# A hybrid decoder step in fp32-grade products: w_o split beside the last S products, transpositions in the rounded 32-bit type, smaller DMA scratch

## The chip, the cores and the metric

One Trainium2 chip; the kernel runs on one of its cores. The metric is device time in microseconds (us), the median of several runs. Engines are called as in the profile: PE is TensorE, PEld its weight loads, DVE VectorE, ACT ScalarE, POOL GpSimd, SP SyncE. L12 is line 12 of the kernel before, unless the change is spoken of.

## The reference, cut to what matters

1024 prompt tokens and 64 sample tokens (8 x 8), model width 1024, inner width 2048, 32 heads in 4 groups, state 128, chunks of 128 tokens. All values are 32-bit floats.

```python
proj = h @ w_in                       # h: normed, conditioned x
u_pool, z_pool, z_ssm, xbc, dt_raw, g_raw = split(proj)
p = (pool_mix(u_pool) * silu(z_pool)) @ w_pool_out
...                                   # causal conv, then per chunk and group:
cb  = einsum('bign,bjgn->bijg', C, B)
att = cb[..., None] * decay * dt
y   = einsum('bijge,bjgep->bigep', att, x) + C @ (exp(acs) * h)
h   = h * exp(last) + einsum('bjgn,bjge,bjgep->bgepn', B, w_in, x)
...
s = rmsnorm((y + D * x) * silu(z_ssm), ssm_norm_g) @ w_ssm_out
m = sigmoid(g_pool) * p + sigmoid(g_ssm) * s
x = x + gate * (m @ w_o)              # then the final rmsnorm
```

## The kernel before, in words

**Split products.** A full-precision product is made of three products in the rounded 32-bit type (F32R, "fp32r" in the profile; TensorE takes it in one pass, while a plain 32-bit product shows as two passes): each operand is split into a high part (its rounded copy, made by ACT) and a low part (the rest, a subtraction on DVE or POOL), and high x high, high x low and low x high are accumulated. `gemm_` (L348 to L356) does this for one 128-row output tile in blocks of 384, 352 and 352 columns (1088 tokens), three matmuls for each 128 of depth; its PSUM tiles `mm` come from a pool of three. A transposition on TensorE is a matmul whose stationary operand is the data and whose streamed operand is an identity matrix.

**Stages.** Up to about 830 us: projections, convolution and the samples' recurrence. From about 832 to 1120 us the chunk stage: 4 groups x 8 chunks of the recurrence (`chunk`), woven with the products that don't need the last group: 8 units of P (`P_unit`, with w_pool_out) and 24 units of S for groups 0 to 2 (`S_unit`, with w_ssm_out). From about 1122 us the tail: 8 units of S for group 3 (`tail_unit`), then the product with w_o (8 row tiles of 48 matmuls and the sample rows), about 1204 to 1291 us, and the final norm.

**A chunk.** SP loads x, B, C (`xb`) and the decays (`dec`); ACT takes exponentials of dec (L1196, L1392, the latter for `cE`), POOL masks it (L1187). TensorE transposes four tiles of x (L1400) and one of B (L1402) and multiplies B by C (L1403, a plain 32-bit product). ACT copies B's high part (`bt`, L1406) and, once DVE has scaled x (L1412, L1413), the high part of x (`xw`, L1415). DVE multiplies dec and cE by the product of B and C (L1416, L1418) and makes the low parts `xwl` (L1419) and `btl` (L1420). Then TensorE makes the outputs of the heads (`inner`, L1208 with dec, L1211 with cE) and the new state (L1429 to L1431), and `finish` gates the output and splits it for the S products (L1362 to L1373).

**Split of w_o, before.** From the 14th chunk on, `wo_splits` runs between the steps of the chunks in 16 halves of 128 x 512: SP loads a half into `pw` (2 buffers), ACT copies its high part into `ph` (1 buffer, L1674) and issues its store to HBM (L1675), POOL subtracts in place (L1676), and SP stores the low part (L1670). In the tail `wo_prep` (L1761, L1762) loads both parts of each of the 8 row blocks again.

**A tail unit.** After the three blocks of unit m, `m_done` (L1783) has DVE add the block to the sums of groups 0 to 2 (L1795), multiply by the gain (sigmoid gate times the row norm, `r`, L1788, then L1800) and POOL add P's part (L1801; DVE does it for m = 7). `m_split` splits the result m for the last product: ACT copies (L1779), DVE subtracts (L1780), and L1768 and L1769 do the same for the 64 sample columns `sh`. `samples[m]` are four matmuls of 512 columns with w_o for the sample rows (L1774).

**Order.** Each engine works in order. A scheduler sets each engine's order from the program by priorities; `in_line` chains the instructions of the named engines in program order instead. In the chunk stage it holds for TensorE; `high_priority(PRIO)` moves work ahead in the scheduler.

Of the kernel before, what the change touches and what calls it, by code (L numbers as in the profile page):

```python
# [8 lines left out]
F32 = mybir.dt.float32  # L9
# [37 lines left out]
def tile_pool_ssd_step(  # L47
# [65 lines left out]
    make_identity(nc, ident)  # L113
    blk = const([NS, NB], "blk")
# [1267 lines left out]
    def chunk(g, c):  # L1382
# [16 lines left out]
        for q in range(4):  # L1399
            nc.tensor.transpose(px[:, q * P:(q + 1) * P], xb[:, q], ident)  # L1400
        pbc = PB()
        nc.tensor.transpose(pbc[:, :P], Bf, ident)  # L1402
# [258 lines left out]
    wo_d = [dram(f"wo{k}", [P, 2, D]) for k in range(8)]  # L1661

    def wo_splits():
        raws = {}
        for n in range(18):
            if n < 16:
                raws[n] = ck.tile([P, 512], F32, tag="pw", name=nm("pw"), bufs=2)
                load(raws[n], w_o[0, n // 2 * P:n // 2 * P + P, n % 2 * 512:n % 2 * 512 + 512])
            if n > 1:
                load(wo_d[(n - 2) // 2][:, 1, n % 2 * 512:n % 2 * 512 + 512], raws.pop(n - 2))  # L1670
            yield
            if n < 16:
                hi = ck.tile([P, 512], F32R, tag="ph", name=nm("ph"), bufs=1)
                act(hi, raws[n], AF.Copy)  # L1674
# [3 lines left out]
    wos = wo_splits()  # L1678
# [16 lines left out]
    for i in range(len(seq)):  # L1695
        if i > 12:
            next(wos, None)
# [6 lines left out]
        if i > 12:  # L1704
            next(wos, None)
# [10 lines left out]
    for it in (pc_, wos):  # L1716
        for _ in it:
            pass
# [8 lines left out]
    mq = open_("mq", 5)  # L1727
# [16 lines left out]
    rstd = [PB() for _ in range(3)]  # L1744
    for c in range(9):
# [3 lines left out]
        mm(rstd[c // 4][:, c % 4 * P:c % 4 * P + n], ones[:n, :], dg, start=True, stop=True)  # L1749
# [6 lines left out]
    def wo_prep(k, mem):  # L1756
# [4 lines left out]
        load(hi.bitcast(F32), wo_d[k][:, 0])  # L1761
        load(lo.bitcast(F32), wo_d[k][:, 1])  # L1762
# [20 lines left out]
    def m_done(m):  # L1783
        r = R()
        load(r, gs_d[m])
        for j, ps in enumerate(rstd):
            s = slice(512 * j, min(512 * j + 512, T))
# [158 lines left out]
```

## Time and profile before

| what | value |
|---|---|
| median of 3 runs | 1298.56 us (1297.77 to 1300.59) |
| profiled execution, span | 1297.1 us |
| PE busy | 1255.9 us (97%) |
| DVE / ACT / POOL busy | 910.5 (70%) / 708.8 (55%) / 677.4 (52%) us |
| DMA traffic | 251.70 MB, mean 194 GB/s |
| HBM read / written | 167.06 MB / 83.01 MB |
| chunk stage, first and last transposition of x | 832.8 and 1102.2 us |

A row of the timeline reads: start in us, length in us, engine, line, operation, output<-inputs by the program's names, shapes, number of like instructions joined in the row, and in brackets the time that the engine stood idle before it and what ended that. Rows of groups give the count, then busy us and mean ns of one, then the idle time before them and its releasers. Matmuls overlap, so their cost is read from start to start. The median lies 1.46 us above the profiled span.

### The profile page before, as it was taken

The numbers are of one execution on the slowest core, as the hardware profiler recorded it, in microseconds if no ns is written. First come the engines' busy times: TensorE is split into PE (matmuls) and PEld (weight loads), VectorE is DVE, ScalarE is ACT, GpSimd is POOL, SyncE is SP. The second block draws the span as 40 slices with busy tenths as digits, with TensorE's granted clock in tenths as the row PEclk, the third lists the DMA queues.
The fourth block names the chain that finished last, engine by engine and source line by source line (L and its number), as shares of the span: only waits on it lengthen the run. The fifth ranks groups of instructions, "written<-read, shape, count | busy, mean of one in ns | idle before, by whom it ended". The sixth has DMA issues, their size and how long they took to land.

```text
span 1297.1 us, 26554 instructions
## 1 busy us (share of the span) xinstructions
PE 1255.9 (97%) x9771; PEld 1173.9 (90%) x9771; DVE 910.5 (70%) x1580; ACT 708.8 (55%) x1684; POOL 677.4 (52%) x563
## 2 busy tenths in 40 slices
PE   7999999999999999999999999999998999999998
PEld 6779999989999999999889999889998999999786
DVE  4685778866979578775777665488676888576433
ACT  4665356375656564545455453687987868201111
POOL 1007668677869776664344444276776747314000
PEclk9999999999999999999999999999999999999999
DMA  9837345465455544444656555999988656575631
GB/s 326 259 107 224 119 150 173 142 202 170 146 180 197 165 155 133 161 135 129 181 158 173 152 178 164 356 355 354 338 270 262 202 168 199 172 266 159 226 106 52
DMA packets 233795, 251.70 MB, mean 194 GB/s; under 512 B 31265, under 2 KB 177905, under 8 KB 233658
## 3 DMA queue, kind: packets, MB, share of 16 engines
q1 hardware_dynamic: 161568, 171.60, 42.1%
q10 hardware_dynamic: 72098, 78.41, 17.5%
q8 instruction: 77, 1.26, 0.4%
q14 instruction: 52, 0.43, 0.1%
HBM read 167.06 MB, written 83.01 MB: 193 GB/s over the span
## 4 chain that ended last, share of the span: by engine, by line
PE 67%; issue 8%; DMA 8%; DVE 6%; POOL 5%; ACT 4%; SPq 0%; ACTq 0%; POOLq 0%; DVEq 0%
PE ps L603 6%; PE ps L604 6%; PE ps L605 6%; PE mm L603 6%; PE mm L605 6%; PE mm L604 6%; PE mm L355 3%; PE mm L356 3%; PE mm L354 3%; PE ps L1208 2%; PE ps L1892 2%; PE ps L1894 2%; PE ps L1893 2%; POOL wlo L163 2%; PE ps L1211 2%
## 5 line engine op out<-in xcount | busy, mean ns | idle before, releaser
L163 POOL TENSOR_TENSOR wlo<-rawA,whi 128x512 fp32r<-128x512 f32 x120 | 184.0, 1538 | 185.6 <-ACT whi L160 101.6
L163 POOL TENSOR_TENSOR wlo<-raw,whi 128x512 fp32r<-128x512 f32 x92 | 150.7, 1646 | 125.3 <-ACT whi L160 91.1
L354 PE MATMUL mm<-Y,whi 128*128 128x352 f32 (+1 forms) x480 | 160.1, 334 | 0.7 <-DVE G L1795 0.5
L355 PE MATMUL mm<-Y,whi 128*128 128x352 f32 (+1 forms) x480 | 157.3, 328 | 1.0 <-DVE Y L1466 1.0
L356 PE MATMUL mm<-Y,wlo 128*128 128x352 f32 (+1 forms) x480 | 156.9, 327 | 0.0
L605 PE MATMUL mm<-Y,wlo 128*128 128x272 f32 x496 | 143.6, 290 | 3.9 <-POOL wlo L163 3.1
L603 PE MATMUL ps<-Y,whi 128*128 128x272 f32 x496 | 144.5, 291 | 2.3 <-ACT o L803 1.7
L603 PE MATMUL mm<-Y,whi 128*128 128x272 f32 x496 | 146.5, 295 | 0.2
L604 PE MATMUL ps<-Y,whi 128*128 128x272 f32 x496 | 143.1, 289 | 0.0
L604 PE MATMUL mm<-Y,whi 128*128 128x272 f32 x496 | 142.9, 288 | 0.0
L605 PE MATMUL ps<-Y,wlo 128*128 128x272 f32 x496 | 142.6, 288 | 0.0
L160 ACT ACTIVATE whi<-rawA 128x512 fp32r<-128x512 f32 x125 | 78.2, 626 | 95.6 <-PE ps L604 44.9
L1051 DVE SCALAR_TENSOR_TENSOR GA<-GA,cvT,GA 128x1112 f32<-128x1112 f32 x72 | 127.1, 1769 | 0.6 <-ACT GA L1048 0.5
L160 ACT ACTIVATE whi<-raw 128x512 fp32r<-128x512 f32 x96 | 58.7, 626 | 91.4 <-DVE raw L549 41.7
L605 PEld LDWEIGHTS mm<-Y,wlo 128*128 128x128 f32 x496 | 93.4, 188 | 5.8 <-POOL wlo L163 4.2
L603 PEld LDWEIGHTS ps<-Y,whi 128*128 128x128 f32 x496 | 93.3, 188 | 4.0 <-ACT o L803 1.9
L603 PEld LDWEIGHTS mm<-Y,whi 128*128 128x128 f32 x496 | 93.3, 188 | 2.5 <-issue 0.8
L604 PEld LDWEIGHTS mm<-Y,whi 128*128 128x128 f32 x496 | 93.4, 188 | 0.7 <-issue 0.6
L604 PEld LDWEIGHTS ps<-Y,whi 128*128 128x128 f32 x496 | 93.3, 188 | 0.3 <-issue 0.2
L605 PEld LDWEIGHTS ps<-Y,wlo 128*128 128x128 f32 x496 | 93.4, 188 | 0.2 <-issue 0.2
L354 PEld LDWEIGHTS mm<-Y,whi 128*128 128x128 f32 x480 | 90.3, 188 | 3.2 <-DVE G L1795 1.4
L355 PEld LDWEIGHTS mm<-Y,whi 128*128 128x128 f32 x480 | 90.3, 188 | 3.2 <-DVE Y L1466 1.6
(452 smaller groups left out, 3851.6 us busy)
## 6 DMA issues: line engine op xcount, KB each, us to landing
rawA<-in_w_in SPq DMA_DIRECT2D x46, 512.0 KB
dec<-acs_d SPq DMA_DIRECT2D x32, 512.0 KB
xbc<-GA ACTq DMA_DIRECT2D x24, 512.0 KB
xb<-xbc SPq DMA_DIRECT2D x32, 384.0 KB
rawA<-in_w_in SPq DMA_DIRECT2D x32, 256.0 KB
pw<-in_w_ssm_out ACTq DMA_DIRECT2D x32, 256.0 KB
ws<-ph ACTq DMA_DIRECT2D x32, 256.0 KB
ws<-pw SPq DMA_DIRECT2D x32, 256.0 KB
```

What stands on the lines that cost most here:

```text
L160: ins = act(hi[:, :, :ncols], raw[:, :, :ncols], AF.Copy)
L163: (eng or nc.gpsimd).tensor_tensor(lo[:, :, :ncols], raw[:, :, :ncols], hi[:, :, :ncols].bitcast(F32), ALU.subtract)
L354: mm(ps[:, :n], a, rh[k][:, o:o + n], start=(k == 0), stop=False)
L355: mm(ps[:, :n], a, rl[k][:, o:o + n], start=False, stop=False)
L356: mm(ps[:, :n], b, rh[k][:, o:o + n], start=False, stop=(k == nk - 1))
L603: mm(p, hi, ah, start=(k == 0), stop=False)
L604: mm(p, hi, al, start=False, stop=False)
L605: mm(p, lo, ah, start=False, stop=(k == 3))
L1051: V.scalar_tensor_tensor(d[:, :n], rp[:, k:k + n], cvT[:, 24 * k + mc:24 * k + mc + 1], d[:, :n], ALU.mult, ALU.add)
L1208: mm(o[hh], xd[:S, 2 * q + hh, :], dec[:S, 2 * q + hh], start=True, stop=state is None)
L1211: mm(o[hh], state[:, h * 64:h * 64 + 64], cE[:, h], start=False, stop=True)
L1892: mm(ps[:, :cw], mhk, wo[k][0][:, s], start=(k == 0), stop=False)
```

## The change

Five things change.

1. `wo_splits` and its 8 MB of HBM buffers go. In the tail, unit m loads the raw 128 x 1024 rows of block m of w_o into an M tile (`wo_load`), and for m < 6 ACT copies the high part and POOL subtracts the low one (`wo_split`); blocks 6 and 7 follow after the units, with block 7's subtraction on DVE.
2. The transpositions of x and B in the chunk stage are declared in the rounded 32-bit type (`turn_r`), data, identity and output alike, with an identity of its own made by POOL at the start. The transpositions of the state (L1239, L1448) stay as they are.
3. The scratch memory for DMA descriptors is 1024 instead of 16384 bytes for each partition, and the pool M of 4352-byte tiles in the tail has 8 buffers instead of 5. The diagonals of the norms lie in one M tile instead of four small ones.
4. The gain (three instructions on DVE) is made when the last block of a unit is there, for m < 7, instead of ahead of the unit's products in the program.
5. In the tail TensorE and DVE are held to program order. The split of m comes one unit later, and the sample products two units later, without their high priority.

```diff
+    identR = const([P, P], "identR", F32R)
+    nc.gpsimd.tensor_copy(identR, ident)
+    def turn_r(out, src):
+        nc.tensor.transpose(out.bitcast(F32R), src.bitcast(F32R), identR)
...
-            nc.tensor.transpose(px[:, q * P:(q + 1) * P], xb[:, q], ident)
+            turn_r(px[:, q * P:(q + 1) * P], xb[:, q])
...
-        nc.tensor.transpose(pbc[:, :P], Bf, ident)
+        turn_r(pbc[:, :P], Bf)
...
-    def wo_splits():
-        raws = {}
-        for n in range(18):
-            if n < 16:
-                raws[n] = ck.tile([P, 512], F32, tag="pw", name=nm("pw"), bufs=2)
-                load(raws[n], w_o[0, n // 2 * P:n // 2 * P + P, n % 2 * 512:n % 2 * 512 + 512])
-            if n > 1:
-                load(wo_d[(n - 2) // 2][:, 1, n % 2 * 512:n % 2 * 512 + 512], raws.pop(n - 2))
-            yield
-            if n < 16:
-                hi = ck.tile([P, 512], F32R, tag="ph", name=nm("ph"), bufs=1)
-                act(hi, raws[n], AF.Copy)
-                store_(wo_d[n // 2][:, 0, n % 2 * 512:n % 2 * 512 + 512], hi.bitcast(F32))
-                nc.gpsimd.tensor_tensor(raws[n].bitcast(F32R), raws[n], hi.bitcast(F32), ALU.subtract)
-            yield
...
-    mq = open_("mq", 5)
+    mq = open_("mq", 8)
...
-        dg = sm.tile([P, P], F32, tag="stc", name=nm("dg"), bufs=4)[:n, :n]
+        dg = dgs[:n, c * P:c * P + n]
...
+    def wo_load(k):
+        raws[k] = M((P, D))
+        load(raws[k], w_o[0, k * P:(k + 1) * P, :])
+
+    def wo_split(k, mem):
         if k < 4:
             hi, lo = w4[0][:, k, :D], w4[1][:, k, :D]
         else:
             hi, lo = mem((P, D), F32R), mem((P, D), F32R)
-        load(hi.bitcast(F32), wo_d[k][:, 0])
-        load(lo.bitcast(F32), wo_d[k][:, 1])
+        raw = raws.pop(k)
+        act(hi, raw, AF.Copy)
+        (V if k == 7 else nc.gpsimd).tensor_tensor(lo, raw, hi.bitcast(F32), ALU.subtract)
...
-            if m < 5:
-                wo_prep(m, M)
-            if m < 7:
-                m_split(m, M8 if m < 4 else G)
-            if m < 5:
-                with tc.high_priority(PRIO):
-                    samples[m]()
+            wo_load(m)
+            if m < 6:
+                wo_split(m, M)
+            if m > 0:
+                m_split(m - 1, M8 if m < 5 else G)
+            if m > 1:
+                samples[m - 2]()
+    in_line((mybir.EngineType.PE, mybir.EngineType.DVE), True)
     run_units([tail_unit(m) for m in range(8)])
...
-    for k in (5, 6):
-        wo_prep(k, late)
-        samples[k]()
-    wo_prep(7, late)
+    for k in (6, 7):
+        wo_split(k, late)
+    samples[6]()
     m_split(7, late)
+    in_line((mybir.EngineType.PE, mybir.EngineType.DVE))
...
-    nc = _bacc.Bacc("TRN2", target_bir_lowering=False, num_devices=1)
+    nc = _bacc.Bacc("TRN2", target_bir_lowering=False, num_devices=1, dynamic_dma_scratch_size=1024)
```

The rows below are the order of one engine, before and after, with the tiles' buffer numbers; "x5" is five like instructions in a row. First ACT in the chunk stage, around the first chunk of group 2, where S products of group 0 are made (G is their sum, L1636 its copy from PSUM; the other names are those of a chunk). Before:

```order
L1674 ACTIVATE ph_14588<-pw_14542 128x512
L1636 ACTIVATE G_13145<-mm_13146 128x384
L1196 ACTIVATE dec_13114<-dec_13114,acT 128x128 x5
L1636 ACTIVATE G_13145<-mm_13190 128x352
L1196 ACTIVATE dec_13114<-dec_13114,acT 128x128 x3
L1675 DMA wo_11233<-ph_14588 128x512
L1406 ACTIVATE bt_13173<-ps_13170 128x128
L1674 ACTIVATE ph_14720<-pw_14674 128x512
L1415 ACTIVATE xw_13179<-ps_13165 128x512
L1423 ACTIVATE xD_13299<-xb_13112,Dv 128x128 x4
L1675 DMA wo_11234<-ph_14720 128x512
```

After (lines six further down in the code):

```order
L1642 ACTIVATE G_13127<-mm_13128 128x384
L1202 ACTIVATE dec_13096<-dec_13096,acT 128x128 x8
L1642 ACTIVATE G_13127<-mm_13169 128x352
L1412 ACTIVATE bt_13152<-ps_13149 128x128
L1421 ACTIVATE xw_13158<-ps_13144 128x512
L1429 ACTIVATE xD_13271<-xb_13094,Dv 128x128 x4
```

The copy of w_o's half that stood between the copies bt and xw, and the two store issues, are gone; the rest keeps its order. Second, POOL in the tail, from the addition of unit 0 on (G is a unit's sum, m P's part). Before:

```order
L1801 TENSOR_TENSOR G_12288<-G_12288,m_15440 128x1088
L1801 TENSOR_TENSOR G_12415<-G_12415,m_15508 128x1088
L1801 TENSOR_TENSOR G_12570<-G_12570,m_15576 128x1088
L1801 TENSOR_TENSOR G_12696<-G_12696,m_15644 128x1088
L1849 TENSOR_TENSOR half_15985<-ident 128x64 x2
L1801 TENSOR_TENSOR G_12883<-G_12883,m_15712 128x1088
L1801 TENSOR_TENSOR G_13015<-G_13015,m_15782 128x1088
```

After (L1753 is the subtraction of w_o, its outputs Y for blocks 0 to 3 and m for 4 and 5; L1796 the addition):

```order
L1753 TENSOR_TENSOR Y_15298<-m_15360,Y_15297 128x1024
L1753 TENSOR_TENSOR Y_15298<-m_15419,Y_15297 128x1024
L1796 TENSOR_TENSOR G_12282<-G_12282,m_15311 128x1088
L1753 TENSOR_TENSOR Y_15298<-m_15485,Y_15297 128x1024
L1753 TENSOR_TENSOR Y_15298<-m_15555,Y_15297 128x1024
L1796 TENSOR_TENSOR G_12409<-G_12409,m_15370 128x1088
L1753 TENSOR_TENSOR m_15628<-m_15625,m_15627 128x1024
L1796 TENSOR_TENSOR G_12564<-G_12564,m_15436 128x1088
L1753 TENSOR_TENSOR m_15700<-m_15697,m_15699 128x1024
L1796 TENSOR_TENSOR G_12690<-G_12690,m_15506 128x1088
```

Six subtractions now stand among the first four additions, two of them ahead of the first. Third, DVE in the tail around unit 4 of the change (L1789 is the addition from PSUM, L1780 the gain, L1795 the multiplication by it, L1760 and L1771 the split of unit 3's m):

```order
L1789 TENSOR_TENSOR G_12877<-mm_15578,G_12877 128x384
L1789 TENSOR_TENSOR G_12877<-mm_15592,G_12877 128x352
L1789 TENSOR_TENSOR G_12877<-mm_15606,G_12877 128x352
L1780 TENSOR_TENSOR R_15574<-ps_15275,R_15574 128x512
L1780 TENSOR_TENSOR R_15574<-ps_15276,R_15574 128x512
L1780 TENSOR_TENSOR R_15574<-ps_15277,R_15574 128x64
L1795 TENSOR_TENSOR G_12877<-G_12877,R_15574 128x1088
L1760 TENSOR_TENSOR sh_15631<-G_12690,sh_15631 128x64
L1771 TENSOR_TENSOR m_2641_15635<-G_12690,m_2640_15634 128x1024
```

Each unit is now three additions, the gain, the multiplication, and the split of the unit before it; before, the gain of the next unit stood between the additions of a unit.

More of the change, by code (lines that the diff above doesn't have):

```diff
@@ L1695, in tile_pool_ssd_step @@
     for i in range(len(seq)):
-        if i > 12:
-            next(wos, None)
         if i + 1 < len(seq):
@@ L1703, in tile_pool_ssd_step @@
             next(seq[i - 1], None)
-        if i > 12:
-            next(wos, None)
         next(seq[i], None)
@@ L1715, in tile_pool_ssd_step @@
     next(seq[-1], None)
-    for it in (pc_, wos):
-        for _ in it:
-            pass
+    for _ in pc_:
+        pass
     in_line((mybir.EngineType.PE,))
@@ L1785, in m_done, with gains @@
         load(r, gs_d[m])
-        for j, ps in enumerate(rstd):
-            s = slice(512 * j, min(512 * j + 512, T))
-            V.tensor_tensor(r[:, s], ps[:, :s.stop - s.start], r[:, s], ALU.mult)
+        def gains():
+            for j, ps in enumerate(rstd):
+                s = slice(512 * j, min(512 * j + 512, T))
+                V.tensor_tensor(r[:, s], ps[:, :s.stop - s.start], r[:, s], ALU.mult)
+        if m == 7:
+            gains()
         mt = M()
```

6 lines of the change are left out of this document (3 added, 3 removed).

## The prediction

> **What bounds the kernel now.** I read the busy shares first, then a table of busy time by stage, then the timeline of TensorE around each loss. The page's first part gives one engine that is nearly always at work:
>
> ```profile
> PE 1255.9 (97%) x9771; PEld 1173.9 (90%) x9771; DVE 910.5 (70%) x1580; ACT 708.8 (55%) x1684; POOL 677.4 (52%) x563
> ```
>
> TensorE is the bound as a whole, but the share is a mean over stages. The table by windows (length, then busy time and instructions of PE, PEld, DVE, ACT and POOL, granted clock, DMA share, GB/s) covers the chunk stage (832 to 1120 us) and the tail:
>
> ```profile
> core 0: us, PE busy (x) PEld busy (x) DVE busy (x) ACT busy (x) POOL busy (x), PEclk, DMA share, GB/s
> 850.00:900.00 50.00, 47.03 (x388) 43.57 (x387) 42.46 (x64) 41.91 (x118) 35.65 (x37) 1.00 1.03 357
> 900.00:950.00 50.00, 49.96 (x414) 46.34 (x413) 36.53 (x57) 44.11 (x119) 34.62 (x38) 1.00 0.99 328
> 950.00:1000.00 50.00, 45.42 (x369) 41.94 (x368) 34.01 (x48) 42.09 (x119) 36.04 (x40) 1.00 0.87 276
> 1000.00:1050.00 50.00, 49.96 (x423) 46.24 (x422) 43.03 (x70) 38.95 (x110) 32.28 (x39) 1.00 0.68 199
> ...
> 1150.00:1200.00 50.00, 49.34 (x282) 46.70 (x282) 38.36 (x62) 8.44 (x14) 21.05 (x9) 1.00 0.62 199
> ```
>
> The clock is full throughout. TensorE loses 2.97 us in 850 to 900 and 4.58 us in 950 to 1000, together 7.55 us; in between it is full even with the DMA engines at 0.99. So two things can be gained here: those holes, and shorter work on TensorE itself. The timeline of PE (start, length, instruction, idle before it and who ended it) shows most of it at three places, in five holes:
>
> ```profile
> 857.18 0.44 PE L1208 MATMUL ps<-dec,xd 128*64 128x128 f32 x4 [1.40 <-DVE dec L1416]
> 858.40 0.44 PE L1211 MATMUL ps<-cE,hst 128*64 128x128 f32 x4 [0.78 <-POOL Y L1373]
> ...
> 983.19 0.50 PE L1429 MATMUL ps<-xw,bt 128*128 128x512 f32 x1 [2.05 <-DVE xwl L1419]
> ...
> 991.75 0.44 PE L1208 MATMUL ps<-dec,xd 128*64 128x128 f32 x4 [0.89 <-DVE dec L1416]
> 992.88 0.44 PE L1211 MATMUL ps<-cE,hst 128*64 128x128 f32 x4 [0.69 <-DVE cE L1418]
> ```
>
> They add to 1.40 + 0.78 + 2.05 + 0.89 + 0.69 = 5.81 us. Behind each stands VectorE, and behind VectorE stands ScalarE. Its timeline, and then the row of VectorE ahead of the first hole:
>
> ```profile
> 847.16 0.63 ACT L1674 ACTIVATE ph<-pw 128x512 fp32r<-128x512 f32 x1 [3.28 <-DMA pw<-in_w_o]
> ...
> 981.30 0.63 ACT L1674 ACTIVATE ph<-pw 128x512 fp32r<-128x512 f32 x1 [2.75 <-DMA wo<-ph]
> 981.83 0.58 ACT L1415 ACTIVATE xw<-ps 128x512 fp32r<-128x512 f32 x1
> ```
>
> ```profile
> 855.90 1.22 DVE L1416 TENSOR_TENSOR dec<-dec,ps 128x1024 f32<-128x1024 f32 x1 [2.23 <-ACT dec L1196]
> ```
>
> L1674 is the first half of a split of w_o. Twice it held ScalarE, which works in order: 3.28 us for its raw rows to arrive, and 2.75 us for the one ph buffer to be stored. In the second case L1415 (xw), which the product L1429 at 983.19 needs through L1419, stands right behind it. In the first, the exponentials L1196 come late, L1416 waits 2.23 us for them, and PE waits for L1416. The 991 holes follow the second wait by 10 us, on the same chain of dec.
>
> **The change part by part.**
>
> *Splits of w_o out of the chunk stage.* ScalarE loses 16 copies of 0.63 us and the two waits, POOL 16 subtractions, the queues 4 MB read and 8 MB written; the reload of 8 MB in the tail becomes one read of 4 MB. Moved past SP's queue are 16 loads of pw and 16 stores of the low halves, past ScalarE's 16 stores. None of this is on TensorE: it counts only through the holes. The order of TensorE in the chunk stage is the same otherwise. If the waits go, what is next late is VectorE, busy 36.5 to 43 of 50 us, or the decay loads. I take 4.5 of the 5.81 us, because the 991 pair lies at one remove from the wait (a copy of 0.63 us still precedes its chain, but the load on VectorE stays). Bounds: all of the 7.55 us, and on the other side a new wait of the size of the largest hole, a loss of 2.05.
>
> *Transpositions.* There are 5 per chunk (four of x at L1400, one of B at L1402), 32 chunks. PE's timeline, in the middle of dense work, with 352-column products ahead; then, from an earlier stage, products of 272 columns ahead of transpositions of a 64-column operand; then the weight loads by line (count, busy us, mean ns):
>
> ```profile
> 987.52 0.32 PE L355 MATMUL mm<-Y,whi 128*128 128x352 f32 x1
> 987.68 0.33 PE L356 MATMUL mm<-Y,wlo 128*128 128x352 f32 x1
> 987.85 0.60 PE L1400 MATMUL ps<-ident,xb 128*128 128x128 f32 x4
> 988.28 0.27 PE L1402 MATMUL ps<-ident,xb 128*128 128x128 f32 x1
> 988.39 0.39 PE L1403 MATMUL ps<-xb 128*128 128x128 f32 x2
> ```
>
> ```profile
> 598.66 0.29 PE L604 MATMUL ps<-Y,whi 128*128 128x272 f32 x1
> 598.79 0.29 PE L605 MATMUL ps<-Y,wlo 128*128 128x272 f32 x1
> 598.91 0.60 PE L1239 MATMUL ps<-ident,hst 128*64 128x128 f32 x4
> ```
>
> ```profile
> L1400 PEld LDWEIGHTS ps<-ident,xb 128*128 128x128 f32 x128 | 15.9, 140 | 0.9
> ...
> L1403 PEld LDWEIGHTS ps<-xb 128*128 128x128 f32 x64 | 9.7, 191 | 0.0
> ```
>
> Matmuls overlap, so a start-to-start step is the cost. Five transpositions take 988.39 - 987.85 = 0.54 us, 0.108 each. Products in the rounded type step 0.13 us at 272 columns and 0.16 at 352, 0.03 for 80 columns, so 0.4 ns a column and some 14 ns besides: 128 columns would be about 0.067. No row shows a rounded transposition. Bound on the cheap side: 5 x 0.041 x 32 = 6.6 us less. On the dear side: the load could set the step and grow from 140 to the 191 ns of a plain one; if a quarter of those 51 ns shows, 160 x 0.013 = 2 us more. I take 5.0 less, near the cheap end. The nearest row is L1239: its operand has 64 weight columns instead of 128, and four take 0.60 us all the same, so the streamed identity and not the weights sets 0.108. From 6.6 I take about 1.3 for L1403, whose full-precision weights are loaded beside L1402 and lose 0.04 us of cover in each of 32 chunks, and 0.3 for transpositions that fall in holes.
>
> Against this stands a row in which the load alone can be what counts, nine products of one streamed column, in two passes each:
>
> ```profile
> 1138.47 2.05 PE L1740 MATMUL ps<-ones,sq_acc 128*128 128x1 f32 x18
> ```
>
> They step (2.05 - 0.24) / 17 = 0.106 us, the same as a transposition. [...]
>
> *The tail.* Eight units of products (36 products and 4 of a sample, at 50.00 / 282 = 0.177 us each: 7.1 us a unit), each ended by VectorE (L1795, L1788, L1800, L1780) and POOL (L1801). The change adds to POOL seven subtractions of 128x1024 and to VectorE one, and puts VectorE in program order. ScalarE has room for eight copies (8.44 of 50 us busy); each waits for its raw rows, and behind it on ScalarE stand the copies of m, on which VectorE's L1780 and then the sample products wait. At the tail's 199 GB/s 512 KB take 2.6 us, and eight loads 21 us of the 57 that eight units last, so I count no wait there. POOL's and VectorE's timelines, then VectorE's groups over the tail:
>
> ```profile
> 1154.66 2.54 POOL L1801 TENSOR_TENSOR G<-G,m 128x1088 f32<-128x1088 f32 x1 [32.64 <-DVE G L1800]
> ```
>
> ```profile
> 1153.29 1.29 DVE L1800 TENSOR_TENSOR G<-G,R 128x1088 f32<-128x1088 f32 x1
> ...
> 1155.50 2.85 DVE L1800 TENSOR_TENSOR G<-G,R 128x1088 f32<-128x1088 f32 x1
> ```
>
> ```profile
> L1800 DVE TENSOR_TENSOR G<-G,R 128x1088 f32<-128x1088 f32 x7 | 10.6, 1510 | 0.1
> L1788 DVE TENSOR_TENSOR R<-ps,R 128x512 f32<-128x512 f32 x16 | 10.2, 683 | 7.1 <-DMA R<-gs 6.7 <-PE ps L1749 0.4
> L1795 DVE TENSOR_TENSOR G<-mm,G 128x352 f32<-128x352 f32 x16 | 8.1, 518 | 2.2 <-PE mm L356 2.2
> L1780 DVE TENSOR_TENSOR m<-G,m 128x1024 fp32r<-128x1024 f32 x4 | 4.9, 1216 | 0.0
> ```
>
> The multiplication started at 1155.50 ends at 1158.35, 1.15 us after POOL's addition ended at 1157.20: it stood still while POOL worked. [...] In a unit VectorE has 1.29 + 1.22 us and some 0.2 of that kind, POOL 2.54 + 2.54 x 1024/1088 = 4.93: together 7.6 us, 0.5 more than PE's 7.1. Two of the seven subtractions can run in POOL's 32.64 idle us; over the units of the other five the surplus is 2.5 us, part of it hidden by the three PSUM buffers of the products. I take 1.5 us more. Bounds: the holes of today's tail could close (50.00 - 49.34, so 0.7 less; I take 1), or all seven units could show the surplus, 7 x 0.5 = 3.5 more.
>
> *The rest.* Identity in the rounded type: one copy on POOL, which at the start waits for nothing later than PE's first product; one tile for the diagonals, smaller scratch (no transfer of this kernel is issued by POOL): nothing. Their cover is POOL's idle start; without it, one short copy, below 0.5 us.
>
> **Sum.** The profiled execution spans 1297.1 us, 1.46 below the median of 1298.56; the terms are differences, so they are put to the median. 1298.56 - 4.5 - 5.0 + 1.5 = 1290.56; I say **1290.5 us**.
>
> **Rivals.**
>
> *Transpositions keep their step* (the load sets it, or the declared type does nothing to a transposition): for it L1740's 0.106, against it L1239. 1290.5 + 5.0 = 1295.5 us. Chance 0.28.
>
> *The holes stay and only change their releaser*: with ScalarE free, the decay loads or VectorE end the wait last. For it, one hole of the five is put down to POOL, and VectorE has 42.46 of 50 us busy in 850 to 900; against it, 900 to 950 is full at 44.11 us of ScalarE and a DMA share of 0.99. 1290.5 + 4.5 = 1295.0 us. Chance 0.10. Both of these at once: 1300 us, chance 0.05.
>
> *Slower: POOL's subtractions block VectorE in its fixed order.* A two-input instruction that meets a POOL one waits up to 2.4 us, and the evictions behind it wait too. It decides once VectorE is more than three product blocks (3 x 12 x 0.16 = 5.8 us) behind, since then no PSUM buffer is free. With all seven on the path: 7 x 2.4 = 16.8 us in place of the 1.5, 1290.5 - 1.5 + 16.8 = 1305.8 us. [...] Chance 0.10.
>
> **How the numbers follow.** The forecast has 0.47, its own range 1286.2 to 1294.1 (1298.56 - 6.6 - 5.8 with a free tail, or 1298.56 - 4.0 - 3.5 with the tail at 3.0, a bit over half of what I take and most of the tail's bound). The range 1285.5 to 1298.5 takes in both single rivals and most of what lies beside them and leaves out the double one and the slow one. A measurement of this kernel can tell 0.2%, 2.6 us: 1295.96 and 1301.16. Faster: the forecast, nearly two thirds of the two single rivals, 0.69. Slower: the slow rival and some of the double one, 0.12. Within: 0.19.
>
> **What would show it.** Right: PE's steps at the transpositions of about 0.067 us; no ScalarE wait above 1 us in 840 to 1000, and the two windows above 49 us; the holes of the tail no more than some 2 us in all. Wrong: transpositions at 0.108; holes of the same size at L1208, L1211 or L1429 with a DMA or VectorE behind; or PE waiting for L1795's successor on VectorE while POOL runs a subtraction.

## The result and the profile after

The changed kernel takes 1298.89 us (median of 20 runs, 1292.0 to 1303.8), the kernel before 1298.71 us (20 runs, 1295.12 to 1303.14): a ratio of 1.0001, 95% interval 0.999 to 1.0012. Nothing changed that can be measured; 1290.5 us was forecast. The work did shrink: 16.8 MB less is moved, and of the two windows that had the holes one is full now. The profiled execution of the kernel after was one of its longer ones, 2.9 us above its median (1301.8 us); rows and stages below are of that one.

The page of the kernel after, its busy shares and its traffic:

```profile
PE 1258.6 (97%) x9771; PEld 1177.4 (91%) x9771; DVE 913.3 (70%) x1581; ACT 709.5 (55%) x1676; POOL 682.1 (52%) x555
...
HBM read 158.67 MB, written 74.62 MB: 179 GB/s over the span
```

Its table by windows, with the columns of the prediction's:

```profile
850.00:900.00 50.00, 46.85 (x389) 43.29 (x388) 41.14 (x63) 40.34 (x116) 29.94 (x33) 1.00 0.95 318
900.00:950.00 50.00, 46.49 (x366) 42.30 (x364) 32.58 (x51) 36.94 (x102) 24.23 (x27) 0.97 0.66 207
950.00:1000.00 50.00, 49.88 (x418) 46.61 (x417) 36.15 (x55) 43.64 (x123) 32.40 (x39) 1.00 0.68 211
...
1150.00:1200.00 50.00, 45.58 (x260) 44.09 (x259) 45.60 (x60) 11.26 (x16) 36.37 (x14) 0.97 0.62 218
```

TensorE's hole in 950 to 1000 is gone (45.42 to 49.88). The one in 850 to 900 is not (47.03 to 46.85), 900 to 950 has a new one (49.96 to 46.49) though the DMA engines fell to 0.66 there, and the tail lost 3.8 us (49.34 to 45.58). The granted clock is below 1 in the two windows that got worse. Rows of the kernel after carry its own line numbers: in the chunk stage they are six higher (L1214 is L1208), in the tail L1765 is the samples' L1774, L1760 and L1771 are the split's L1769 and L1780, L1789 and L1795 are L1795 and L1800, L1796 is POOL's L1801, L1753 is the new subtraction, and L118 is `turn_r`. The larger holes in TensorE's timeline, with what ended them:

```profile
857.98 0.44 PE L1214 MATMUL ps<-dec,xd 128*64 128x128 f32 x4 [1.74 <-DVE dec L1422]
859.20 0.44 PE L1217 MATMUL ps<-cE,hst 128*64 128x128 f32 x4 [0.78 <-DVE cE L1424]
...
915.34 0.43 PE L361 MATMUL mm<-Y,whi 128*128 128x352 f32 x1 [1.63 <-POOL Y L1379]
...
931.85 0.44 PE L1214 MATMUL ps<-dec,xd 128*64 128x128 f32 x4 [0.78 <-DVE dec L1422]
933.08 0.44 PE L1217 MATMUL ps<-cE,hst 128*64 128x128 f32 x4 [0.79 <-DVE cE L1424]
...
1161.76 1.17 PE L1765 MATMUL ps<-Y,sh 128*128 128x512 f32 x4 [1.76 <-DVE sh L1760]
...
1165.59 0.69 PE L360 MATMUL mm<-Y,whi 128*128 128x384 f32 x1 [2.66 <-DVE G L1789]
```

Executions of one and the same code differ before the chunk stage begins (818.82 against 816.75 us in the first row below), so I compare stages and not ends. TensorE makes the same 9771 matmuls in both, so their starts can be set side by side by number:

| in the profiled execution | before | after |
|---|---|---|
| start of matmul 6501 (same code up to here) | 816.75 | 818.82 |
| from there to matmul 9001 (chunk stage) | 321.56 | 318.67 |
| from there to the last one (tail) | 152.06 | 155.83 |
| holes of 0.15 us and more in the chunk stage, from 830 us on | 9.01 | 6.72 |
| the same in the tail | 0.85 | 4.42 |

The chunk stage gained 2.9 us where 9.5 were forecast, and the tail lost 3.8 where 1.5 were. (A hole of 1.04 us ahead of 830 us stands in every run.)

These are single executions, and more of the same order are on record. In the chunk stage the runs e4, e5, e6, e8 and e11 below have the kernel after's order on DVE, ACT and POOL; their stages last 316.06 to 318.42 us, with holes of 4.9 to 6.8 us. In the tail e2 and e7 have its order, and the first of the two holes (1.76 us) is missing in both: 2.66 and 2.68 us of holes, and a tail that is 2.3 us longer than before. So with this order the chunk stage gains 2.9 to 5.5 us against the one execution of before, and the tail loses 2.3 to 3.8.

**The transposition's step.** TensorE's timeline around the transpositions of a chunk, from the last product ahead of them to the second one behind, before and then after:

```profile
843.24 0.34 PE L356 MATMUL mm<-Y,wlo 128*128 128x384 f32 x1
...
844.35 0.33 PE L355 MATMUL mm<-Y,whi 128*128 128x352 f32 x1
```

```profile
843.91 0.34 PE L362 MATMUL mm<-Y,wlo 128*128 128x384 f32 x1
844.09 0.54 PE L118 MATMUL ps<-identR,xb 128*128 128x128 f32 x5
844.46 0.46 PE L1409 MATMUL ps<-xb 128*128 128x128 f32 x2
844.68 0.41 PE L360 MATMUL mm<-Y,whi 128*128 128x352 f32 x1
844.92 0.32 PE L361 MATMUL mm<-Y,whi 128*128 128x352 f32 x1
```

1.11 us before, 1.01 after: 0.10 us in a chunk (the median over all 32 chunks is 1.109 against 1.010), 3.2 us in all. A rounded transposition steps 0.37 / 5 = 0.074 us here (0.076 in the median chunk) instead of 0.108. The plain product of B and C behind it (L1409) takes 0.22 instead of 0.15 us up to the next product (medians 0.21 and 0.14).

**The tail.** DVE's timeline of the kernel after, then POOL's, at the two holes:

```profile
1156.00 3.31 DVE L1795 TENSOR_TENSOR G<-G,R 128x1088 f32<-128x1088 f32 x1
1159.23 2.38 DVE L1760 TENSOR_TENSOR sh<-G,sh 128x64 fp32r<-128x64 f32 x1
1161.54 3.53 DVE L1771 TENSOR_TENSOR m<-G,m 128x1024 fp32r<-128x1024 f32 x1
1164.99 1.41 DVE L1789 TENSOR_TENSOR G<-mm,G 128x384 f32<-128x384 f32 x3
```

```profile
1153.25 2.55 POOL L1796 TENSOR_TENSOR G<-G,m 128x1088 f32<-128x1088 f32 x1 [1.23 <-DVE G L1795]
1155.75 5.78 POOL L1753 TENSOR_TENSOR Y<-m,Y 128x1024 fp32r<-128x1024 f32 x2
1161.49 2.49 POOL L1796 TENSOR_TENSOR G<-G,m 128x1088 f32<-128x1088 f32 x1
```

Two subtractions of w_o (L1753) follow each other on POOL. Three instructions of DVE take 3.31, 2.38 and 3.53 us while POOL is at work; in the profile of before, with POOL idle, the same three take 1.29, 0.22 and 1.22 (L1800 at 1153.29, L1769 at 1179.86, L1780 at 1180.42 us). In the texts below this waiting beside POOL is called the lock; how the two engines come to it is not shown. The first samples' product waits for sh (1.76 us). Behind the third stand three evictions (L1789), TensorE has no PSUM buffer left, and waits 2.66 us.

The forecast had two subtractions in POOL's idle time ahead of the first addition, and there they are. But it counted no wait for the raw rows of w_o, and ACT's timeline and POOL's show one:

```profile
1145.84 1.06 ACT L1752 ACTIVATE Y<-m 128x1024 fp32r<-128x1024 f32 x1 [5.69 <-DMA m<-in_w_o]
```

```profile
1146.97 2.42 POOL L1753 TENSOR_TENSOR Y<-m,Y 128x1024 fp32r<-128x1024 f32 x1 [26.13 <-ACT Y L1752]
```

POOL stands idle for 26.13 us, and when the first copy by ACT releases it, the first addition is only 6 us away: no third subtraction fits ahead of it.

**The clock.** Four windows of 3.4 us each: the one with the hole at 915 and its successor, the last ahead of 1165.3 and its successor.

```profile
912.70:916.10 3.40, 1.58 (x8) 0.95 (x7) 2.02 (x4) 3.40 (x12) 3.40 (x5) 1.00 0.64 234
916.10:919.50 3.40, 3.40 (x13) 3.40 (x13) 2.71 (x4) 2.10 (x6) 0.60 (x1) 0.51 0.78 194
1161.90:1165.30 3.40, 1.03 (x4) 0.50 (x4) 3.40 (x2) 1.20 (x2) 3.40 (x2) 1.00 1.04 368
1165.30:1168.70 3.40, 3.11 (x10) 3.11 (x11) 3.37 (x7) 0.00 (x0) 2.00 (x1) 0.50 0.43 149
```

Behind these two holes the granted clock is 0.5 for 3.41 us (from 916.13 and from 1165.31 us), which by my estimate costs up to 3.41 / 2 = 1.7 us more each; behind the holes at 858 us (1.74 and 0.78) it stays at 1. The profiled execution of before has no such stretch until its last 6 us; over all runs its mean granted clock is 0.9962 (104 runs beside the experiments), that of the kernel after 0.9940 (20 runs).

### The profile page after: what moved, and what is told of

Same layout as the page of the kernel before. It is cut to its first block, busy times and chain, and to the rows that moved or that the text cites. A ratio compares the mean times of both kernels' runs of the same rounds, so it can differ in the third digit from the quotient of the medians.

```text
span 1300.1 us, 26439 instructions
## 1 busy us (share of the span) xinstructions
PE 1258.6 (97%) x9771; PEld 1177.4 (91%) x9771; DVE 913.3 (70%) x1581; ACT 709.5 (55%) x1676; POOL 682.1 (52%) x555
## 4 chain that ended last, share of the span: by engine, by line
PE 75%; DVE 6%; DMA 6%; issue 5%; ACT 4%; POOL 3%; ACTq 0%; SPq 0%; POOLq 0%; DVEq 0%
PE ps L609 6%; PE ps L610 6%; PE ps L611 6%; PE mm L609 6%; PE mm L611 6%; PE mm L610 6%; PE mm L361 5%; PE mm L360 5%; PE mm L362 5%; PE ps L1214 2%; PE ps L1888 2%; PE ps L1890 2%; PE ps L1889 2%; POOL wlo L169 2%; PE ps L1217 2%
```

## The experiments

The theory after the result (A in most of the texts below): the forecast gains are there, but the smaller work comes with a new static order of the chunk stage that has holes of its own; and in the tail POOL's subtractions lock DVE out, which TensorE pays with 3.6 us of waits and a stretch at half clock. Rivals: TensorE's gains are lost to the chain of dec in any case; the fixed order of DVE, and not the lock, makes the tail's holes. Ratios are to before on the same chip; medians of different runs come from different chips, where before's own median lies between 1298.71 and 1299.2 us. Stages and holes are those of one profiled execution of each.

| run | median us | ratio to before, 95% | chunk stage | holes chunk / tail | mean clock |
|---|---|---|---|---|---|
| kernel after | 1298.89 | 1.0001 (0.999 to 1.0012) | 318.67 | 6.7 / 4.4 | 0.9940 |
| e1_turn_only | 1306.39 | 1.005 (1.0035 to 1.0065) | 328.58 | 15.5 / 0.8 | 0.9923 |
| e2_plain_turn | 1300.33 | 1.0011 (0.999 to 1.0031) | 318.33 | 4.5 / 2.7 | 0.9950 |
| e3_no_wo_split | 1296.85 | 0.9974 (0.996 to 0.9989) | 317.03 | 4.5 / 1.6 | 0.9970 |
| e4_no_subtract | 1292.43 | 0.9943 (0.9921 to 0.9965) | 316.84 | 6.8 / 0 | 0.9972 |
| e5_dve_free | 1295.97 | 0.9983 (0.9963 to 1.0003) | 317.26 | 5.8 / 1.8 | 0.9956 |
| e6_early_splits | 1299.62 | 1.0004 (0.9984 to 1.0024) | 316.06 | 4.9 / 4.4 | 0.9934 |
| e7_dec_four | 1310.37 | 1.0073 (1.0045 to 1.0101) | 327.34 | 11.4 / 2.7 | 0.9902 |
| e8_subtract_dve | 1302.95 | 1.0021 (1.0004 to 1.0038) | 318.42 | 5.4 / 6.9 | 0.9958 |
| e9_z_early | 1298.1 | 0.9997 (0.998 to 1.0014) | 319.47 | 6.2 / 2.2 | 0.9939 |
| e10_plain_dve_free | 1299.61 | 1.0011 (0.9993 to 1.0028) | 318.65 | 6.1 / 2.1 | 0.9953 |
| e11_adds_first | 1295.24 | 0.9978 (0.9963 to 0.9992) | 316.88 | 5.6 / 1.1 | 0.9955 |
| e12_scratch_only | 1308.9 | 1.0073 (1.0055 to 1.0092) | 331.39 | 12.2 / 0.9 | 0.9917 |
| e13_turn_15872 | 1303.01 | 1.0032 (1.0016 to 1.0049) | 324.93 | 11.4 / 0.6 | 0.9951 |

### The chunk stage: what each part brings alone

**The split of w_o alone.** From the kernel before, `wo_splits` is taken out; the tail's loads take other split weights.

```diff
-        load(hi.bitcast(F32), wo_d[k][:, 0])
-        load(lo.bitcast(F32), wo_d[k][:, 1])
+        load(hi.bitcast(F32), ws_d[0][k].rearrange("p s k c -> p (s k c)"))
+        load(lo.bitcast(F32), ws_d[1][k].rearrange("p s k c -> p (s k c)"))
```

> The kernel before without the split of w_o in the chunk stage; the tail loads other split weights of the same size in place of w_o, so the last product isn't the reference's. Theory A (only the holes at 980 to 993 us and the one at 839 hang on the split; others appear where the decay or gate loads come late in SP's queue): the holes of the chunk stage fall from 9.0 to between 6 and 7.5 us, the time by 2 to 3 us, some 1296. The prediction on record: 4.5 us less, 1294. Rival B (the holes are the chain's own and only change their releaser): no change, 1298 to 1299.

Its table by windows:

```profile
850.00:900.00 50.00, 48.88 (x410) 45.17 (x407) 41.98 (x67) 41.64 (x117) 31.35 (x34) 1.00 0.93 310
900.00:950.00 50.00, 48.33 (x402) 44.21 (x401) 34.85 (x54) 39.45 (x107) 26.12 (x30) 1.00 0.72 227
950.00:1000.00 50.00, 50.00 (x398) 46.90 (x396) 36.36 (x55) 42.38 (x119) 31.81 (x40) 1.00 0.67 206
```

Holes of 4.5 us instead of 9.0, a chunk stage of 317.03 instead of 321.56 us: 4.5 us, the prediction's term to the tenth, and more than I expected after the result. The agreement is luck in part. Of the five holes that the prediction counted (5.81 us) 4.76 us are gone, the 991 pair among them, which it had meant to leave; three more (884, 962 and 980 us, 1.74 us) went as well, and 1.96 us opened at 929 and 1069 us, where 900 to 950 was full before. The time fell by 2.3 us (1296.85 against 1299.2), with an interval that takes in 4.5.

**The transpositions alone.** To the kernel before, `turn_r` and its identity are added; they need 512 bytes in a partition that are not free, so the scratch is made smaller as in the change.

> The kernel before with the rounded transpositions (and the smaller scratch, which makes room for their identity) and nothing else of the change. Theory A (a rounded transposition saves 0.10 us in each of 32 chunks, as read from the trace of the changed kernel, and the saving reaches the end): 3.2 us faster than before, some 1295.5. The prediction on record took 5.0 us. Rival B (what TensorE saves in a chunk it waits for in the next, because the chunk stage is set by the chain of dec through POOL, ACT and DVE): 0 to 1 us faster, with longer holes before L1208 and L1211.

Neither: 7.2 us slower. The dense step is shorter by the same 0.10 us, but two holes of 4.59 and 5.48 us stand at the start of the chunk stage. Two runs were added to tell the reason. One has the smaller scratch and nothing else:

```diff
-    nc = _bacc.Bacc("TRN2", target_bir_lowering=False, num_devices=1)
+    nc = _bacc.Bacc("TRN2", target_bir_lowering=False, num_devices=1, dynamic_dma_scratch_size=1024)
```

> The kernel before with the smaller DMA scratch and nothing else: no instruction added or taken away, but the tiles lie at other addresses, and the scheduler orders the chunk stage anew (316 of ACT's lines of order differ, none of TensorE's). Theory A (a new static order opens or closes holes of several us by itself, and this is what made the rounded transpositions alone 7 us slower): 3 to 8 us slower than before, with holes of 3 us or more at the start of the chunk stage. Rival B (it was the transpositions, the order is harmless): 1298 to 1300, holes as before.

TensorE's timeline there:

```profile
843.26 1.97 PE L1208 MATMUL ps<-dec,xd 128*64 128x128 f32 x16 [3.86 <-DVE dec L1416]
...
867.80 0.69 PE L1208 MATMUL ps<-dec,xd 128*64 128x128 f32 x4 [5.36 <-DVE dec L1416]
```

Not one instruction is new, and the kernel is 10.1 us slower, more than A's 3 to 8: tiles at other addresses, another order, holes of 3.86 and 5.36 us, and half clock behind them (mean clock 0.9917). At the second hole DVE waits 3.52 us for ACT's exponentials (L1196), which start only at 864.01 us. The holes grew by 3.2 us (9.0 to 12.2); the stretches at half clock in this stage, 17.1 us together, can cost up to 8.5 us more, so in this execution the clock may be the larger part of the 9.8 us that the stage lost. Slower transfers are not the reason: in this stage the packets of the larger DMA queue (q1) took 71.3% of 322 us before and 68.9% of 332 us here, 230 and 229 us of the 16 engines' time, for 73.45 and 73.22 MB. Whether the addresses act only through the order isn't shown. With the transpositions on the same scratch (e1), in yet another order, it is 2.5 us faster than that. The other run has the transpositions with 15872 bytes of scratch, a third order:

> The kernel before with the rounded transpositions and a scratch that is only 512 bytes smaller, as much as their identity needs: a third order of the chunk stage. Theory A (the order decides): the step at the transpositions again 0.10 us shorter in each chunk, but the holes of the chunk stage other than the 9.0 us of before and the 17 us with the small scratch, and the time follows the holes: before's time, minus 3.2, plus the change of the holes. Rival B (rounded transpositions cost some 7 us whatever the order): 1305 to 1307.

The holes are 11.4 us, the chunk stage 324.93 us. By A's rule 321.56 - 3.2 + 2.4 would be 320.8; two stretches at half clock (at 842.7 and 979.2 us, up to 3.4 us together) make it 324.2. So the order counts, with the clock as a second term that A lacked; the median, 4.2 us above before, lies 5 us above A's rule and 2 us below B's range, and neither text had it.

**The changed kernel with plain transpositions**, with DVE in fixed order and without:

```diff
-        nc.tensor.transpose(out.bitcast(F32R), src.bitcast(F32R), identR)
+        nc.tensor.transpose(out, src, ident)
```

> The changed kernel with the transpositions back in plain 32-bit. Theory A: 3.2 us slower than the changed kernel, some 1302. Rival B (the saving is lost again in waits): within 1 us of the changed kernel, 1299.

> The changed kernel without the fixed order of DVE and with plain 32-bit transpositions. Theory A (a rounded transposition saves 0.10 us in a chunk, 3.3 us in all, and is lost only where the new schedule opens holes of TensorE): dense stretches 0.10 us a chunk slower than with rounded ones, total 1 to 3 us above 1296. Rival B (rounded transpositions bring nothing to the end): 1295 to 1296.5.

1300.33 against 1298.89 us (1.4 us, within what the runs can't tell), and 1299.61 against e5's 1295.97 (3.6 us, more than A's 1 to 3, with intervals that still touch). In the profiled pair e2 and after the chunk stages are equal, 318.33 and 318.67: the 3.2 us came back as holes, 6.7 against 4.5 us. In e5 and e10 the holes are alike (5.8, 6.1) and the stage differs by 1.4 us with a stretch at half clock in e5. Over all executions of these two orders, the stage with rounded transpositions lasts 316.06 to 318.67 us (six, mean 317.4) and with plain ones 318.33 and 318.65: about 1 us of the 3.2 is seen there. That the rest goes into holes and the clock is likely, and not shown.

**Where the new holes come from.** ACT's timeline of the kernel after ahead of the hole at 915, then POOL's:

```profile
904.16 1.06 ACT L1398 ACTIVATE cE<-dec 128x1024 f32<-128x1024 f32 x1 [5.38 <-DMA dec<-acs_d]
```

```profile
905.30 1.64 POOL L1193 TENSOR_SCALAR_AFFINE_SELECT dec<-dec 128x1024 f32<-128x1024 f32 x1 [6.25 <-ACT cE L1398]
...
907.62 1.28 POOL L1379 TENSOR_TENSOR Y<-v,Y 128x512 fp32r<-128x512 f32 x1
...
912.26 1.09 POOL L1193 TENSOR_SCALAR_AFFINE_SELECT dec<-dec 128x1024 f32<-128x1024 f32 x1 [2.94 <-PE ps L1214]
...
914.01 1.27 POOL L1379 TENSOR_TENSOR Y<-v,Y 128x512 fp32r<-128x512 f32 x1
```

ACT stands in order before dec, POOL's mask behind ACT, and the low part of the S product's input (L1379) behind the mask. One chunk later the mask waits for the products with this late dec (912.26), and the low part behind it, ready at 915.28, ends TensorE's hole at 915.34. So I gave dec a fourth buffer:

```diff
-        dec = ckt([P, 8, P], "dec", 3)
+        dec = ckt([P, 8, P], "dec", 4)
```

> The changed kernel with four buffers for the decays (dec) in the chunk stage instead of three. Theory A (with w_o's transfers gone the holes at 857, 867, 913 and 931 us come from dec and z loads that stand late in SP's queue, where dec waits for a buffer: 12.8 us in 880 to 935 us): the holes of the chunk stage fall from 6.7 to 3 us or less, 3 to 5 us faster than the changed kernel. Rival B (each new schedule has holes of its own, whatever the buffers): holes of 5 us or more at other places, within 2 us of the changed kernel either way.

Rival B: 11.4 us of holes at other places (3.56 us at 837, 3.92 at 860), 11.5 us slower than before. B had the holes, and not their price: it said within 2 us of the kernel after. The profiled execution (1302.69 us) was the shortest of this run, 7.7 us below its median, so its holes are not those of the median. The other attempt moved the load of z one step ahead, with DVE free:

```diff
+        if g + c > 0:
+            sz = ckt([P, 4, P], "sz", 3)
+            load(sz, z_d[g][:, :, o:o + P])
         if c > 0:
             cE = ckt([P, 8, P], "cE")
```

> The changed kernel without the fixed order of DVE (as in the run before that had it so, 1295.97) and with the load of z issued a step earlier in each chunk. Theory A (the hole of 1.75 us at 855 us is z arriving late: ACT waits 3.28 us for the product with z, and the exponentials of the next dec stand behind it): the holes at 855 us shrink from 2.5 to under 1 us, 1 to 3 us faster than 1296. Rival B (SP's queue is only shifted, so dec or x arrive later in turn): holes of the same sum, 1295 to 1298.

Rival B again, 0.1 us above its range: 2.01 and 0.78 us at 856. My reading of that hole was wrong: in the kernel after DVE works without a pause from 842.55 us until it comes to the product with z at 847.27, so z was not what it waited for.

### The tail: lock, order or work

**No w_o subtraction at all**: the low part is a second copy by ACT.

```diff
-        (V if k == 7 else nc.gpsimd).tensor_tensor(lo, raw, hi.bitcast(F32), ALU.subtract)
+        act(lo, raw, AF.Copy)
```

> The changed kernel in which the low part of w_o is a second copy by ACT and not a subtraction, so that POOL and DVE have no w_o work in the tail (the last product isn't the reference's). Theory A (POOL's subtractions lock DVE out, and DVE in its fixed order makes TensorE wait 4.4 us at the sample products): the two holes of 1.76 and 2.66 us go, and with them the stretch at half clock that follows: 4 to 6 us faster than the changed kernel, 1293 to 1295. Rival B (the fixed order of DVE or the later split of m makes the holes, POOL does not matter): holes of 3 us or more stay, less than 1.5 us faster.

Its row of the table by windows:

```profile
1150.00:1200.00 50.00, 50.00 (x283) 47.60 (x283) 40.97 (x71) 19.23 (x28) 23.94 (x9) 1.00 0.66 215
```

No hole is left, with DVE in the same fixed order and m split as late: 1292.43 us, 6.5 below the kernel after and slightly beyond A's 4 to 6. The subtractions make the tail's loss, and rival B falls. ACT has eight copies more here, so the work of the split as such isn't gone, only that of POOL and DVE.

**DVE not held to program order** (`in_line` with PE alone in the tail):

> The changed kernel without the fixed order of DVE in the tail (TensorE keeps its own). Theory A (POOL's subtractions lock DVE out; in the fixed order the evictions stand behind a locked instruction): an eviction can now go ahead in the scheduler's order, which doesn't know of the lock; the two holes of 4.4 us shrink to 1.5 to 3 us, 1296 to 1298. Rival B (the fixed order alone makes the holes): no hole above 0.6 us, as in the kernel before, and 1292 to 1294.

One hole of 1.24 us and two of some 0.25 remain, 1295.97 us, as A expected (its range began 0.03 us higher). So the fixed order adds to the loss: evictions have to stand behind a locked instruction. It isn't all of it, since 1.76 us are left against 0.85 before; and against the 2.66 us of the kernel after's order in e2 and e7 the gain is under 1 us.

**All subtractions on DVE:**

```diff
-        (V if k == 7 else nc.gpsimd).tensor_tensor(lo, raw, hi.bitcast(F32), ALU.subtract)
+        V.tensor_tensor(lo, raw, hi.bitcast(F32), ALU.subtract)
```

> The changed kernel with all eight subtractions of w_o on DVE and none on POOL. Theory A (the lock, not the work): DVE has 1.2 us more in a unit, 7.1 us against TensorE's 7.1, and only POOL's additions lock it; holes of 2 us or less, 2 to 4 us faster than the changed kernel. Rival B (DVE's total work in a fixed order is what counts): holes of 4 us or more, the changed kernel's time or slower.

Rival B. TensorE's timeline at the sample products:

```profile
1156.68 1.16 PE L1765 MATMUL ps<-Y,sh 128*128 128x512 f32 x4 [1.03 <-DVE sh L1760]
...
1165.30 1.21 PE L1765 MATMUL ps<-Y,sh 128*128 128x512 f32 x4 [0.91 <-DVE sh L1760]
```

A unit now lasts 8.6 to 8.9 us, not 7.1: ten small holes, 6.9 us in all. My sum of DVE's work (7.1 us) counted no wait beside POOL's additions; how much of the 1.5 to 1.8 us is that wait is not shown.

**Blocks 0 to 3 split ahead of the units:**

```diff
+    for k in range(4):
+        wo_load(k)
+        wo_split(k, M)
     in_line((mybir.EngineType.PE, mybir.EngineType.DVE), True)
...
-            wo_load(m)
-            if m < 6:
-                wo_split(m, M)
+            if m < 4:
+                wo_load(m + 4)
+            if m < 2:
+                wo_split(m + 4, M)
```

> The changed kernel with the loads and splits of blocks 0 to 3 of w_o ahead of the tail's units, where POOL stood idle for over 20 us, and those of blocks 4 and 5 in units 0 and 1. The chunk stage and the orders of TensorE and DVE are those of the changed kernel. Theory A (the lock): with four of six subtractions done before POOL's first addition, the holes at the sample products fall from 4.4 to under 1.5 us and the half-clock stretch behind them goes: 4 to 6 us faster than the changed kernel, 1293 to 1295. Rival B (order or the late split of m): holes of 4 us stay, 1298 to 1300.

POOL's timeline, then TensorE's:

```profile
1140.07 10.56 POOL L1753 TENSOR_TENSOR Y<-m,Y 128x1024 fp32r<-128x1024 f32 x4 [25.13 <-ACT Y L1752]
1150.59 3.58 POOL L1796 TENSOR_TENSOR G<-G,m 128x1088 f32<-128x1088 f32 x1
```

```profile
1156.71 2.04 PE L1765 MATMUL ps<-Y,sh 128*128 128x512 f32 x4 [2.62 <-DVE sh L1760]
```

The holes stayed (4.4 us), as rival B had it, but not for its reason. The raw rows of w_o arrive only at 1138.9 us, so the four subtractions fill POOL until 1150.6, and the addition of unit 0, whose factor DVE had ready at 1146.0, stands behind them for 4.6 us. The idle time that I had counted on lay before the data.

**Additions first**: POOL in program order instead of DVE, two blocks ahead of the units, block m + 2 behind the addition of unit m.

```diff
-    in_line((mybir.EngineType.PE, mybir.EngineType.DVE), True)
+    in_line((mybir.EngineType.PE, mybir.EngineType.Pool), True)
+    for k in range(2):
+        wo_load(k)
+        wo_split(k, M)
...
-            wo_load(m)
-            if m < 6:
-                wo_split(m, M)
+            if m < 6:
+                wo_load(m + 2)
+            if m < 4:
+                wo_split(m + 2, M)
```

> The changed kernel with POOL instead of DVE held to program order in the tail, blocks 0 and 1 of w_o split ahead of the units and block m + 2 behind the addition of unit m, so that one subtraction at most stands between two additions. Theory A (the hole comes from two subtractions in a row that lock DVE and hold the next addition): no hole of TensorE above 1 us in the tail, 1293 to 1296. Rival B (POOL and DVE together are overbooked, 7.6 us against 7.1 a unit, wherever the subtractions stand): holes of 2.5 us or more in all, 1296 to 1299.

TensorE's holes in the tail are down to these:

```profile
1164.41 0.45 PE L360 MATMUL mm<-Y,whi 128*128 128x384 f32 x1 [0.60 <-DVE G L1789]
1169.14 0.42 PE L360 MATMUL mm<-Y,whi 128*128 128x352 f32 x1 [0.46 <-DVE G L1789]
```

1295.24 us, ratio 0.9978 (0.9963 to 0.9992), as theory A had it, and a version that computes everything and is faster than the kernel before. By medians it is 3.7 us below the kernel after. The run changes two things, though: it also frees DVE, as e5 does, and e5 alone has 1295.97 us and 1.8 us of holes. What the place of the subtractions adds, 0.7 us of each, can't be told from noise.

## Why the prediction was wrong, step by step

- **"The rest ... smaller scratch ...: nothing."** This step failed outright. e12 has nothing but the smaller scratch and is 10 us slower than before. The forecast took each part as a difference to a fixed order of ACT, DVE, POOL and SP ("The order of TensorE in the chunk stage is the same otherwise" is true, and not enough); with the tiles at other addresses the scheduler made another order, with holes of its own. In the six executions with the kernel after's order the holes are 4.9 to 6.8 us where e3 has 4.5: 0.4 to 2.3 us given back. By the stage itself, e3's 317.03 less 3.2 would be 313.8 us and those six last 316.06 to 318.67, so holes and clock together gave back 2.2 to 4.8 us. The 10 us are the price in before's program, not in the changed one. How much of this is the scratch's and how much that of the other parts stays open: no run has the change with the old scratch.
- **"Splits of w_o out of the chunk stage", 4.5 us less.** The mechanism held and the size came out, in part by luck: e3, the kernel before without the split, has a chunk stage shorter by 4.5 us, but not by the holes that the forecast had kept and dropped. The cause named for the hole at 857 us held only in part: in e3 0.27 of the 1.40 us is left, but in the kernel after, which has no split there either, the hole is back (1.74 us) and ACT waits as long as before, for DVE:

```profile
847.98 0.63 ACT L1369 ACTIVATE sz<-v 128x512 f32<-128x512 f32 x1 [3.28 <-DVE v L1368]
```

- **"Transpositions", 5.0 us less.** The mechanism held, since the step did fall and the first rival (0.108 kept, by L1740) is refuted by 0.074. The size was off: 0.10 us in a chunk, 3.2 us. A step of 0.076 instead of 0.067 takes 1.4 us of the 6.6, and L1409 took 0.07 us more in a chunk instead of 0.04, 2.2 us instead of 1.3; that this is the exposed load, as the forecast had it, is a reading that no run tests.
- **"The tail", 1.5 us more.** Here the mechanism held, DVE's instructions waiting beside POOL's (3.31 us instead of 1.29), and the size did not: 1.8 to 3.6 us more of holes. The sum of 7.6 against 7.1 us a unit takes the two engines' times as adding up throughout, which no run shows, and is a mean over units; what the trace shows is one place where two subtractions and an addition in a row held three instructions of DVE up for 2.02 + 2.16 + 2.31 = 6.5 us. "I count no wait there", for the raw rows, was wrong as well: ACT waited 5.69 us for the first, so that of POOL's idle time no more than the last part was used. What this wait costs by itself is not shown; e6, with earlier loads, still got its rows only at 1138.9 us. The slower rival's point of decision, no PSUM buffer left, is what ended the hole of 2.66 us; its price of 16.8 us was far too high.
- **"The clock is full throughout."** It was, in that one execution. After two of the kernel after's holes a stretch at 0.5 followed, so a hole may cost more than its length: the mean clock of 0.9940 against 0.9962 is 0.0022 x 1297 = 2.9 us of full clock, if all of it falls on dense work.

Together: -4.5 (split), -3.2 (transpositions), +0.4 to +2.3 (holes of the new order), +1.8 to +3.6 (tail), and up to +2.9 (clock) give -5.5 to +1.1 us; +0.2 was measured, near the upper end. The terms come from single executions, before's from one alone, and the small waits below 0.15 us are in none of them. So the runs show where the forecast gain went, and leave each share open by some 2 us.

Two slips of the working don't move its sum: VectorE's "36.5 to 43 of 50 us" leaves out the 34.01 of 950 to 1000, the window with the largest loss, and 0.47 with nearly two thirds of 0.38 is some 0.72, not 0.69.

## What to carry to other kernels

Where a scheduler orders the engines, a change of memory layout can be a change of order: test it alone before anything is charged to the work that moved, compare stages by TensorE's own instructions, not ends, and take more than one execution of each. Count a hole of TensorE with the stretch of half clock that may follow it (here 3.41 us, twice). And when work goes to POOL beside a DVE that evicts PSUM, look at the longest run of POOL instructions between two that others wait for (here three, which held DVE up for 6.5 us), not at the sums.

## What the runs showed of the hardware

In the profiled execution of the kernel after, the granted clock is 0.5 in four stretches of 3.41 us, from 55.98, 666.96, 916.13 and 1165.31 us, and once more from 1298.43 us, at the end; in that of before only from 1293.35 us, behind the last matmul. In the stretch from 666.96 us products of 272 columns step 0.23 us, ahead of it 0.13. In the 3.41 us right ahead of the four, TensorE was busy for 1.75, 1.00, 1.59 and 1.03 us. Such idle time did not always bring one: in 856.0 to 859.4 us of the kernel after TensorE was busy for 0.88 of 3.40 us, in 980.5 to 983.9 us of before for 1.35, and in the 3.40 us behind each the clock was 1.00. What decides is not shown.

The fastest and the slowest run of equal code on one chip lie 4 to 13 us apart, and the stretches are likely one reason; over the 104 runs of before, time and mean clock go together only loosely (correlation -0.58). That the holes are the cause of the stretches is an inference from the order in time; no run filled a hole with other work to try it.

A transposition declared in the rounded type steps 0.074 us (after, L118) instead of 0.108 (before, L1400 and L1402) at 128 streamed columns, with the same median of 140 ns for its weight load in both profiles (L118 and L1400). A load of equal length goes with two steps, which speaks against the load as what set the plain one.
